# Narrow expert outputs summed in SBUF by one-hot products instead of scatters to HBM

## The chip, the core and the metric

The kernel runs on one core of a Trainium2 chip. The metric is the device time of one execution in microseconds (us); lower is better. The engines are TensorE (PE in the rows, with PEld for its weight loads), VectorE (DVE), ScalarE (ACT), GpSimd (POOL) and SyncE (SP). SP issues most transfers, POOL the indexed ones; all transfers run on the same 16 DMA engines.

## What is computed

One post-norm encoder layer over 512 tokens of width 1024: a token mixer, a cross-attention, and a mixture of experts. Only the last of these matters here:

```python
def moe(x, router_w, router_bias, e_w_gate, e_w_up, e_w_down, s_w_gate, s_w_up, s_w_down):
    scores = jax.nn.sigmoid((xf @ router_w).astype(jnp.float32))
    _, top_e = lax.top_k(scores + router_bias.astype(jnp.float32), TOP_K)   # 8 of 64 experts
    ...
    def body(acc, blk):
        rows, g, e = blk
        xb = x_pad[rows]
        yb = swiglu(xb, e_w_gate[e], e_w_up[e], e_w_down[e]) * g[:, None]
        return acc.at[rows].add(yb), None
    ...
    out = acc[:n] + swiglu(xf, s_w_gate, s_w_up, s_w_down)
...
h = layer_norm(ALPHA * h + y, ln3_g[l], ln3_b[l])
```

Every expert has three weight matrices of 1 MB (1024 x 256, 1024 x 256, 256 x 1024, float32), so 64 experts bring 192 MB from HBM.

## The kernel before

The experts are sorted by the number of their tokens. `CAPS` gives each rank a fixed number of rows: 128 for the first, two ranks with 160 (the "big" experts, which take two blocks, of 128 and of 32 rows), then 112, 96, 80, and for the last 26 ranks 64 (19 of them) and 48 (7). A block of at most 64 rows is *narrow*. All blocks run one after the other in the order of `seq`; `BIG_AT` says at which two places of that order the big experts stand.

For each block m, POOL gathers the token rows (`gather`, tile `xg`, two blocks ahead), PE transposes them (`rows_x`), multiplies them by gate and up weights, the gated product `hm` is transposed (`expert_h`, tile `ht`) and multiplied by the down weights `wd`, ScalarE copies the result to `y`, and POOL adds the rows of `y` to the sums `acc` in HBM with an indexed, adding transfer (`scatter`). Since all scatters write `acc`, each waits for the one before. The work is interleaved: within block m the down product of block m-1 is done, and the transposes of block m+1.

A wide block (over 64 rows) splits its weights and rows into high and low parts (tiles `whl`, `xt`; ScalarE and VectorE do the split) and multiplies three times in the fast form fp32r (`mm3`, lines 101 to 103). A narrow block multiplies unsplit float32 rows (`xn`) with gate and up side by side in two column halves of PE (`narrow_mm`, line 1280; `narrow_out`, line 1291).

Weights arrive through SP in the order of `seq`. `top_up` lets them be issued `LEAD` = 9 loads (three experts) ahead; each load takes one of 20 slots of 8 KB a partition, which weights, their split parts, outputs `y` and other large tiles share. At the end the four 128-row tiles of `acc` are read back into `h`, normalised and stored. A loop behind the blocks (line 1590) handles experts with more tokens than their rows; here it runs zero times.

The order of the instructions on each engine is fixed when the kernel is built: generators that yield estimated durations are interleaved, and within them a tile scheduler places the instructions.

## Time and profile before

| | |
|---|---|
| median of 3 runs | 1319.0 us (1314.91 to 1319.48) |
| profiled execution | 1310.08 us, of which the span from first to last instruction is 1308.3 us |
| busy share of the span | PE 88%, PEld 69%, DVE 57%, ACT 43%, POOL 34% |
| granted TensorE clock, mean | 0.963 of full speed |
| moved by DMA | 324.67 MB, mean 248 GB/s |
| queue q1 (loads and stores issued by SP) | 275.83 MB, 58.2% of 16 engines' span |
| queue q0 (issued by POOL) | 46.80 MB, 14.8% |

A busy share of PE counts a matmul from its start to a modelled end, so matmuls that follow each other overlap in it; starts are what a duration should be read from. The share of a DMA queue is the time that its packets took, as a share of the time of all 16 engines. The expert part begins near 596 us.

### The profile page before, as it was taken

To read this page: it belongs to the slowest core of one execution; us is meant where nothing else is said; L and a number is where in the kernel's file an instruction comes from. 1 tells how busy PE (TensorE), PEld (TensorE's weight loads), DVE (VectorE), ACT (ScalarE), POOL (GpSimd) and SP (SyncE) were. 2 spreads that over 40 slices of the span, in tenths; PEclk is the share of its full clock that TensorE was granted. 3 is DMA by queue.
4 is the path that set the end of the run, shared out by engine and by line. 5 is a ranking of instruction groups with operands and counts; after the bars stand their busy time and mean duration, and the time that the engine had idled before them with its cause. 6 is when DMAs were issued, how large, how long until landed. Compare 5 with 4: busy or idle time off the path is not lost. (4 is left out here: it accounts for less than half of the span.)

```text
span 1308.3 us, 20859 instructions
## 1 busy us (share of the span) xinstructions
PE 1155.8 (88%) x7768; PEld 908.2 (69%) x7768; DVE 748.5 (57%) x1617; ACT 562.0 (43%) x1006; POOL 439.5 (34%) x288
## 2 busy tenths in 40 slices
PE   3999999999898899889999999999899988897770
PEld 2887778988898898878778777777667544553330
DVE  7168986566865557787767777666465211311114
ACT  3235456644454453335555556555454211321122
POOL 4333444542236343552212323232213222223213
PEclk9999999998999899999999999999999989998995
DMA  7322234463326256688999999999999999999974
GB/s 225 86 74 65 58 103 114 121 202 116 126 67 210 63 185 208 226 332 329 299 289 331 352 347 362 332 359 359 350 367 338 350 347 387 363 363 353 349 279 141
DMA packets 136807, 324.67 MB, mean 248 GB/s; under 512 B 12001, under 2 KB 94945, under 8 KB 111873
## 3 DMA queue, kind: packets, MB, share of 16 engines
q1 hardware_dynamic: 119984, 275.83, 58.2%
q0 software_dynamic: 13632, 46.80, 14.8%
q8 instruction: 62, 1.02, 0.3%
q10 hardware_dynamic: 3088, 0.69, 0.2%
q14 instruction: 41, 0.33, 0.1%
HBM read 288.10 MB, written 35.19 MB: 247 GB/s over the span
## 5 line engine op out<-in xcount | busy, mean ns | idle before, releaser
L95 POOL TENSOR_TENSOR whl<-wraw,whl 128x1024 fp32r<-128x1024 f32 x81 | 195.9, 2419 | 265.4 <-ACT whl L94 239.4
L1244 DVE TENSOR_TENSOR whl<-wraw,whl 128x1024 fp32r<-128x1024 f32 x152 | 182.9, 1231 | 85.7 <-ACT whl L1243 79.6
L1332 POOL DMA_INDIRECT acc<-y,sidx x66 | 104.8, 1587 | 361.5 <-DMA acc<-y,sidx 161.4
L101 PE MATMUL ps<-whl,xt 128*96 128x256 f32 (+4 forms) x640 | 184.3, 288 | 5.6 <-ACT whl L1243 3.9
L103 PE MATMUL ps<-whl,xt 128*96 128x256 f32 (+4 forms) x640 | 179.8, 281 | 1.9 <-DVE xt L95 1.9
L102 PE MATMUL ps<-whl,xt 128*96 128x256 f32 (+4 forms) x640 | 179.6, 281 | 0.6 <-DVE whl L1244 0.6
L1243 ACT CAST whl<-wraw 128x1024 fp32r<-128x1024 f32 x152 | 152.5, 1053 | 27.9 <-DMA wraw<-in_e_w_gate_dram 20.0
L1327 PE MATMUL ps<-wd,ht 128*96 128x512 f32 (+4 forms) x320 | 147.1, 603 | 4.0 <-DVE ht L1315 3.8
L1280 PE MATMUL ps<-wraw,xn 128*64 128x256 f32 (+1 forms) x832 | 116.8, 404 | 27.0 <-DMA wraw<-in_e_w_up_dram 12.2
L1220 POOL DMA_INDIRECT xg<-rows,gidx x66 | 76.5, 1159 | 160.3 <-PE ps L1252 62.5
L1299 ACT ACTIVATE sg<-ps 64x256 f32<-64x256 f32 (+6 forms) x66 | 25.0, 378 | 239.6 <-PE ps L1280 127.1
L94 ACT CAST whl<-wraw 128x1024 fp32r<-128x1024 f32 x91 | 95.4, 1048 | 57.1 <-PE ps L103 46.5
L101 PEld LDWEIGHTS ps<-whl,xt 128*96 128x96 f32 (+4 forms) x640 | 104.3, 163 | 6.8 <-ACT whl L1243 4.1
L103 PEld LDWEIGHTS ps<-whl,xt 128*96 128x96 f32 (+4 forms) x640 | 104.3, 163 | 2.9 <-DVE xt L95 2.6
L1280 PEld LDWEIGHTS ps<-wraw,xn 128*64 128x64 f32 (+1 forms) x832 | 60.6, 140 | 65.0 <-DMA wraw<-in_e_w_up_dram 15.8
L102 PEld LDWEIGHTS ps<-whl,xt 128*96 128x96 f32 (+4 forms) x640 | 104.5, 163 | 1.1 <-DVE whl L1244 0.7
L1327 PEld LDWEIGHTS ps<-wd,ht 128*96 128x96 f32 (+4 forms) x320 | 49.5, 164 | 72.9 <-issue 66.0
L1315 DVE COPY ht<-ps 128x128 f32<-128x128 f32 (+6 forms) x66 | 21.4, 324 | 96.3 <-PE ps L1313 96.3
L1328 ACT COPY y<-ps 96x512 f32<-96x512 f32 (+4 forms) x80 | 46.3, 582 | 68.8 <-PE ps L1327 67.4
L1304 DVE SCALAR_TENSOR_TENSOR hm<-ps,og,sg 64x256 f32<-64x256 f32 (+4 forms) x54 | 36.8, 681 | 58.0 <-ACT sg L1299 48.8
L101 PE MATMUL ps<-xTh,whl 128*128 128x512 f32 (+1 forms) x168 | 65.6, 390 | 0.0
L103 PE MATMUL ps<-xTh,whl 128*128 128x512 f32 (+1 forms) x168 | 63.8, 380 | 0.0
(421 smaller groups left out, 2756.7 us busy)
## 6 DMA issues: line engine op xcount, KB each, us to landing
wraw<-in_e_w_gate_dram SPq DMA_DIRECT2D x64, 1024.0 KB, 18.8
wraw<-in_e_w_up_dram SPq DMA_DIRECT2D x64, 1024.0 KB, 15.7
wd<-in_e_w_down_dram SPq DMA_DIRECT2D x64, 1024.0 KB, 18.0
wraw<-in_w_in_dram SPq DMA_DIRECT2D x21, 512.0 KB, 3.7
wraw<-in_m_wkv_dram SPq DMA_DIRECT2D x16, 512.0 KB, 4.2
wraw<-in_m_wq_dram SPq DMA_DIRECT2D x16, 512.0 KB, 3.9
wraw<-in_m_wo_dram SPq DMA_DIRECT2D x16, 512.0 KB, 3.9
wraw<-in_w_o_dram SPq DMA_DIRECT2D x12, 512.0 KB, 3.5
```

The costliest lines, as they stand in the source:

```text
L94: nc.scalar.copy(hi, src)
L95: eng.tensor_sub(lo, src, hi.bitcast(F32))
L101: nc.tensor.matmul(ps, lhsT=a, rhs=b, start=start, stop=False)
L102: nc.tensor.matmul(ps, lhsT=a, rhs=bl, start=False, stop=False)
L103: nc.tensor.matmul(ps, lhsT=al, rhs=b, start=False, stop=stop)
L1220: nc.gpsimd.indirect_dma_start(out=xg[0:n, :], out_offset=None, in_=rows, in_offset=bass.IndirectOffsetOnAxis(ap=gi[0:n, :], axis=0))
L1243: nc.scalar.copy(hi[v], w[i][v])
L1244: lo_eng.tensor_sub(lo[v], w[i][v], hi[v].bitcast(F32))
L1280: nc.tensor.matmul(ps[HALF * i:HALF * i + n, 0:256], lhsT=xt[:, k, 0:n], rhs=w[i][:, k, :], start=k == 0, stop=k == KD - 1)
L1327: nc.tensor.matmul(ps[0:n, :], lhsT=ht[:, j, 0:n], rhs=wd[:, j, cs], start=j == 0, stop=j == 1)
L1328: nc.scalar.copy(y[0:n, cs], ps[0:n, :])
L1332: nc.gpsimd.indirect_dma_start(out=acc, out_offset=bass.IndirectOffsetOnAxis(ap=si[0:n, :], axis=0), in_=y[0:n, :], in_offset=None, comput ...
```

## The change

Three things change. The outputs of the narrow blocks no longer go to `acc` by scatters. Two consecutive narrow blocks form a pair: their outputs go to one tile `yp` (rows 0 to 63 and 64 to 127), as a high part (ScalarE) and the rest (VectorE); VectorE makes a one-hot matrix `ohs` of 128 rows by 512 tokens from the token numbers, and PE multiplies it with `yp` for each of 4 tiles of tokens and 2 column halves, two products each (high and rest), after which VectorE adds the result to the tile `sums` in SBUF. These 8 steps of a pair are spread over the two blocks behind it by `flush(2)`, called twice in a block. The sums are read once from `acc` (four loads of 0.5 MB, issued by POOL in the third narrow block, behind the last scatter of the wide blocks), and the final normalisation works on them directly. Seven slots are taken once for this and kept. The big experts move from places 30 and 50 to 22 and 32, so that all of the last 26 blocks are narrow. The lead of the weight loads is 10 instead of 9 in the narrow part.

```diff
@@ -38,7 +38,7 @@
 EARLY = 6
 FIRST_LOADS = ((("mo13",), 6), (("sh03",), 2), (("sh13",), 4))
 AHEAD, LEAD = 2, 9
-BIG_AT = (30, 50)
+BIG_AT = (22, 32)
 GRP = 4
 LO = (3, 0, 2, 0)
 PARTS = (2, 2)
@@ -1280,19 +1280,77 @@
                 nc.tensor.matmul(ps[HALF * i:HALF * i + n, 0:256], lhsT=xt[:, k, 0:n], rhs=w[i][:, k, :],
                                  start=k == 0, stop=k == KD - 1)

-    def narrow_out(m, ht, wd, n):
-
-        if m % 2 == 0:
-            Y["y"] = slot([P, 2, D], name="y")
-        y = Y["y"][:, m % 2, :]
+
+    ACC, YP, PAIR, STF, OHS, FL, READY = [], [], {}, {}, {}, [], []
+
+    def start_sums():
+
+        OHS[0] = ohs = slot([P, SEQ], F32R, name="tokens")
+        ohs = ohs[:, None, :]
+        ones_ = slot([P, 3, SEQ], F32R, name="ohs")
+        OHS[1] = [ones_[:, n, :] for n in range(3)]
+        YP.extend(slot([P, 2, D], F32R, name="yp") for _ in range(3))
+        tk = wk([P, SEQ], name="tk")
+        nc.gpsimd.iota(tk, pattern=[[1, SEQ]], base=0, channel_multiplier=0, allow_small_or_imprecise_dtypes=True)
+        nc.vector.tensor_copy(ohs[:, 0, :], tk)
+
+    def load_sums():
+        for u in range(2):
+            a = slot([P, 2, D], name="sums")
+            for t in range(2):
+                nc.gpsimd.dma_start(a[:, t, :], acc[(2 * u + t) * P:(2 * u + t + 1) * P, :])
+                ACC.append(a[:, t, :])
+
+    def one_hot_rows(oh, stf):
+        nc.vector.tensor_scalar(oh, OHS[0].bitcast(F32), stf, None, op0=OP.is_equal)
+
+    def add_sums(oh, yp):
+
+        for t in range(NT):
+            for c in range(2):
+                cs = slice(c * 512, (c + 1) * 512)
+                ps = bank()
+                for l in range(2):
+                    nc.tensor.matmul(ps, lhsT=oh[:, t * P:(t + 1) * P], rhs=yp[:, l, cs], start=l == 0, stop=l == 1)
+                nc.vector.tensor_add(ACC[t][:, cs], ACC[t][:, cs], ps)
+                yield
+
+    def narrow_out(m, ht, wd, n, si):
+
+        i = m - M0
+        p, base = i // 2, HALF * (i % 2)
+        if i % 2 == 0:
+            PAIR[p] = YP[p % 3]
+            STF[p] = small.tile([P, 1], F32, name="stf", bufs=3)
+            if min(blocks[m][2], blocks[m + 1][2]) < HALF:
+                nc.vector.memset(STF[p], -1.0)
+        yp, stf = PAIR[p], STF[p]
+        r = slice(base, base + n)
+        if n < HALF:
+            nc.gpsimd.memset(yp[base + 32:base + HALF].bitcast(F32), 0.0)
         ps = bank()
         for j in range(2):
             for c in range(2):
                 nc.tensor.matmul(ps[HALF * c:HALF * c + n, :], lhsT=ht[:, j, 0:n], rhs=wd[:, j, c * 512:(c + 1) * 512],
                                  start=j == 0, stop=j == 1)
-        for c in range(2):
-            nc.scalar.copy(y[0:n, c * 512:(c + 1) * 512], ps[HALF * c:HALF * c + n, :])
-        return y
+        nc.scalar.copy(stf[r], si[0:n])
+        halves = [(slice(c * 512, (c + 1) * 512), ps[HALF * c:HALF * c + n, :]) for c in range(2)]
+        for cs, v in halves:
+            nc.scalar.copy(yp[r, 0, cs], v)
+        for cs, v in halves:
+            nc.vector.tensor_sub(yp[r, 1, cs], v, yp[r, 0, cs].bitcast(F32))
+        if i % 2:
+            oh = OHS[1][p % 3]
+            one_hot_rows(oh, STF.pop(p))
+            READY.append(add_sums(oh, PAIR.pop(p)))
+
+    def flush(n):
+
+        while n and FL:
+            if next(FL[0], 0) == 0:
+                FL.pop(0)
+            else:
+                n -= 1

     def expert_gate(pg, n=P):
         sg = wk([P, 256], name="sg")
...
@@ -1463,7 +1523,8 @@

     def top_up(used):
         ahead = 16 + used // 2 if "listed" in done else 0
-        while fetched[0] < min(max(used + LEAD, ahead), 3 * NEXP):
+        lead = LEAD + (1 if used > 3 * step_of[blocks[M0][0]] else 0)
+        while fetched[0] < min(max(used + lead, ahead), 3 * NEXP):
             next(g_w)
             fetched[0] += 1

@@ -1480,11 +1541,11 @@

     def finish(m, ht, n, wd, si):
         if narrow(m):
-            y = narrow_out(m, ht, wd, n)
+            narrow_out(m, ht, wd, n, si)
         else:
             for c in range(2):
                 y = expert_out(m, ht, wd, c, n)
-        scatter(y, si, n)
+            scatter(y, si, n)

     def rows_x(m):
         return (narrow_x if narrow(m) else expert_x)(XG.pop(m), blocks[m][2])
@@ -1494,13 +1555,20 @@
     def narrow_block(m, X, xt, gs, si):
         r, _, n, _ = blocks[m]
         step = 3 * step_of[r]
+        if m == M0 + 1:
+            start_sums()
+        if m == M0 + 2:
+            load_sums()
         ps = bank()
         w = W[r]
+        FL.extend(READY)
+        READY.clear()
         narrow_mm(xt, w, n, ps, range(KH))
         yield 0.45 * KH, 0.0
         ht = expert_h(*BEFORE[0][0:2])
+        flush(2)
         narrow_mm(xt, w, n, ps, range(KH, KD))
-        yield 0.9, 0.0
+        yield 1.8, 0.0
         top_up(step + 2)
         sg = expert_gate(ps, n)
         finish(m - 1, ht, *BEFORE[0][1:])
@@ -1509,7 +1577,8 @@
         split_part(m + 1, 0)
         if m + 1 < NB:
             X[m + 1] = rows_x(m + 1)
-        yield 0.8, 0.0
+        flush(2)
+        yield 1.6, 0.0
         lists()
         lists()

@@ -1563,6 +1632,8 @@
         for _ in g_m:
             pass
         finish(NB - 1, expert_h(*BEFORE[0][0:2]), *BEFORE[0][1:])
+        FL.extend(READY)
+        flush(16)

     for u in range(2):
         items += [(load_half(w_o[0], 0, c), out_a(u, c), (f"so{4 * u + 3}",), f"oa{u}{c}", LO[0]) for c in range(4)]
...
+        oh, yp = OHS[1][0], YP[0]
+        one_hot_rows(oh, stf)
...
+            split(yp[:, 0, cs], yp[:, 1, cs], ps)
+        for _ in add_sums(oh, yp):
+            pass
...
     gb = G3[0]
-    h3 = [slot([P, 2, D], name="h") for _ in range(2)]
-    for t in range(NT):
-        nc.sync.dma_start(h3[t // 2][:, t % 2, :], acc[t * P:(t + 1) * P, :])
     st = []
     for t in range(NT):
-        h = h3[t // 2][:, t % 2, :]
+        h = ACC[t]
...
```

What this does to the order on two engines is shown here. PE, a narrow block near the end (before: one of the seven with 48 rows; L1268 transposes `xg`, L1280 gate and up, L1313 transposes `hm`, L1291 the down product of the block before; x counts instructions as written, and each float32 product has two rows in a trace):

```order
L1268 MATMUL ps<-ident,xg 128x48 x8
L1280 MATMUL ps<-wraw,xn 48x256
L1313 MATMUL ps<-ident,hm 128x48 x2
L1291 MATMUL ps<-wd,ht 48x512 x3
L1280 MATMUL ps<-wraw,xn 48x256 x15
L1291 MATMUL ps<-wd,ht 48x512
```

The same in the changed kernel, where L1371 stands for L1313, L1334 for L1291, and L1314 is a one-hot product:

```order
L1268 MATMUL ps<-ident,xg 128x48 x8
L1314 MATMUL ps<-yp,ohs 128x512 x4
L1280 MATMUL ps<-wraw,xn 48x256
L1371 MATMUL ps<-ident,hm 128x48 x2
L1314 MATMUL ps<-yp,ohs 128x512 x4
L1334 MATMUL ps<-wd,ht 48x512 x3
L1280 MATMUL ps<-wraw,xn 48x256 x15
L1334 MATMUL ps<-wd,ht 48x512
```

Eight one-hot products are added to a block, four behind the transposes and four behind the transposed `hm`. In this form, with three quarters of the down product ahead of 15 of the 16 gate and up products, stand the last 13 of the 26 narrow blocks. The ones ahead of them have this form:

```order
L1268 MATMUL ps<-ident,xg 128x64 x8
L1314 MATMUL ps<-yp,ohs 128x512 x4
L1280 MATMUL ps<-wraw,xn 64x256 x12
L1371 MATMUL ps<-ident,hm 128x64 x2
L1314 MATMUL ps<-yp,ohs 128x512 x4
L1280 MATMUL ps<-wraw,xn 64x256 x4
L1334 MATMUL ps<-wd,ht 64x512 x4
```

Here the down product comes last, behind all 16 gate and up products.

VectorE, a narrow block before (`hm` the gated product, `xn` half of the next block's rows, `ht` the transposed `hm`, `og` the gates and the expert's number for a later block):

```order
L1304 SCALAR_TENSOR_TENSOR hm<-ps,og,sg 64x128x2
L1406 COPY og<-gsl 64x1
L1408 COPY og<-order 1x1
L1315 COPY ht<-ps 128x2x64
L1271 COPY xn<-ps 128x256
```

and one of the late ones in the changed kernel, up to the next block's `hm`:

```order
L1362 SCALAR_TENSOR_TENSOR hm<-ps,og,sg 64x128x2
L1271 COPY xn<-ps 128x256
L1315 TENSOR_TENSOR sums<-sums,ps 128x512
L1341 TENSOR_TENSOR yp<-ps,yp 64x512 x2
L1315 TENSOR_TENSOR sums<-sums,ps 128x512
L1305 TENSOR_SCALAR ohs<-tokens,stf 128x512
L1373 COPY ht<-ps 128x2x64
L1466 COPY og<-gsl 48x1
L1315 TENSOR_TENSOR sums<-sums,ps 128x512 x2
L1468 COPY og<-order 1x1
L1326 MEMSET stf 128x1
```

Between `hm` and `ht` of a block there stand now two additions to the sums, two rests of `yp`, and in every second block the one-hot matrix.

On POOL the last scatter is that of the last wide block; the four loads of `sums` follow it with one gather between, and behind them there are only gathers and a few memsets.

## Rows read from the trace of the kernel before

**Rows 1.** Windows: busy us of each engine, granted clock, DMA share, GB/s

```profile
866.00:906.00 40.00, 36.40 (x256) 27.46 (x255) 24.89 (x47) 19.03 (x29) 14.71 (x8) 1.00 1.02 355
...
700.00:1007.00 307.00, 296.08 (x2040) 227.04 (x2038) 201.75 (x379) 164.85 (x250) 87.97 (x58) 0.99 1.02 352
1007.00:1272.00 265.00, 223.08 (x1508) 118.96 (x1506) 51.91 (x154) 58.01 (x121) 62.35 (x52) 0.94 1.00 352
...
1250.00:1252.00 2.00, 1.71 (x16) 0.78 (x12) 0.00 (x0) 0.26 (x1) 0.00 (x0) 1.00 1.03 430
```

**Rows 2.** PE in order of time: the gathered rows' transposes as the narrow part begins, and last

```profile
1007.49 0.71 PE L1268 MATMUL ps<-ident,xg 64*128 64x64 f32 x8
...
1035.95 0.71 PE L1268 MATMUL ps<-ident,xg 64*128 64x64 f32 x8
...
1258.89 0.69 PE L1268 MATMUL ps<-ident,xg 48*128 48x48 f32 x8
```

**Rows 3.** End of the narrow part in order of time: start, us, engine, line

```profile
1266.43 0.38 ACT L1299 ACTIVATE sg<-ps 48x256 f32<-48x256 f32 x1 [2.27 <-PE ps L1280]
...
1268.23 1.92 PE L1291 MATMUL ps<-wd,ht 128*48 128x512 f32 x8 [0.35 <-DVE ht L1315]
...
1281.80 1.35 POOL L1332 DMA_INDIRECT acc<-y,sidx  x1 [3.41 <-DMA acc<-y,sidx]
...
1289.92 1.28 DVE L171 BATCH_NORM_STATS2 st<-h 128x6 f32<-128x512 f32 x2 [21.74 <-DMA h<-acc]
```

**Rows 4.** DMA of 1040 to 1260 us: queue, packets, MB, share of 16 engines; issues

```profile
q1 hardware_dynamic: 9424, 68.64, 80.9%
q0 software_dynamic: 3439, 11.21, 21.1%
...
acc<-y,sidx POOLq DMA_INDIRECT x22, 8.3
xg<-rows,gidx POOLq DMA_INDIRECT x21, 8.8
```

**Rows 5.** PE in order of time: a big expert's blocks, from transposes to transposes

```profile
917.89 1.04 PE L1252 MATMUL ps<-ident,xg 128*128 128x128 f32 x8
...
928.78 0.68 PE L1252 MATMUL ps<-ident,xg 32*128 32x32 f32 x8
...
939.14 0.72 PE L1252 MATMUL ps<-ident,xg 80*128 80x80 f32 x8
```

**Rows 6.** PE in order of time: a narrow block that waits for no weights

```profile
1182.49 2.81 PE L1280 MATMUL ps<-wraw,xn 128*64 128x256 f32 x24 [0.26 <-ACT xn L1273]
...
1186.41 1.89 PE L1291 MATMUL ps<-wd,ht 128*64 128x512 f32 x8
...
1189.19 0.43 PE L1280 MATMUL ps<-wraw,xn 128*64 128x256 f32 x1 [0.26 <-ACT xn L1273]
```

**Rows 7.** PE in order of time: fp32r products of 512 columns in a row

```profile
261.22 0.40 PE L102 MATMUL ps<-aT,vb 128*128 128x512 f32 x1
261.45 0.39 PE L103 MATMUL ps<-aT,vb 128*128 128x512 f32 x1
```

**Rows 8.** DVE by line and shape: count, busy us, mean ns of one

```profile
L1304 DVE SCALAR_TENSOR_TENSOR hm<-ps,og,sg 64x256 f32<-64x256 f32 x19 | 12.8, 672 | 24.7 <-ACT sg L1299 24.6
...
L1271 DVE COPY xn<-ps 128x256 f32<-128x256 f32 x19 | 8.1, 424 | 47.9 <-PE ps L1268 47.9
...
L1315 DVE COPY ht<-ps 128x128 f32<-128x128 f32 x19 | 5.5, 291 | 61.5 <-PE ps L1313 61.5
...
L95 DVE TENSOR_TENSOR xTl<-ps,xTh 128x512 fp32r<-128x512 f32 x8 | 5.3, 680 | 0.0
...
L627 DVE TENSOR_SCALAR pa<-pa,r 128x512 f32<-128x512 f32 x8 | 5.2, 656 | 0.2
```

**Rows 9.** POOL in order of time: scatters as the narrow part begins

```profile
1021.78 1.43 POOL L1332 DMA_INDIRECT acc<-y,sidx  x1 [0.87 <-DMA acc<-y,sidx]
...
1032.41 1.43 POOL L1332 DMA_INDIRECT acc<-y,sidx  x1 [3.01 <-DMA acc<-y,sidx]
```

More of the change, by code (lines that the diff above doesn't have):

```diff
@@ L1395, in encoder_layer @@
     NB = len(blocks)
+    M0 = min(m for m in range(NB) if blocks[m][2] <= HALF and not blocks[m][1])
+    assert all(blocks[m][2] <= HALF and not blocks[m][1] for m in range(M0, NB)) and (NB - M0) % 2 == 0
     W, XG, GS = {}, {}, {}
@@ L1616, in encoder_layer @@
         ht = expert_h(expert_mid(expert_gate(pg), pu, gs))
+        stf = small.tile([P, 1], F32, name="stf", bufs=3)
+        nc.vector.tensor_copy(stf, si)
+        oh, yp = OHS[1][0], YP[0]
+        one_hot_rows(oh, stf)
         for c in range(2):
-            y = expert_out(0, ht, w3[2], c)
-        scatter(y, si)
+            cs = slice(c * 512, (c + 1) * 512)
+            ps = bank()
+            for j in range(2):
+                nc.tensor.matmul(ps, lhsT=ht[:, j, :], rhs=w3[2][:, j, cs], start=j == 0, stop=j == 1)
+            split(yp[:, 0, cs], yp[:, 1, cs], ps)
+        for _ in add_sums(oh, yp):
+            pass
     gb = G3[0]
-    h3 = [slot([P, 2, D], name="h") for _ in range(2)]
-    for t in range(NT):
-        nc.sync.dma_start(h3[t // 2][:, t % 2, :], acc[t * P:(t + 1) * P, :])
     st = []
     for t in range(NT):
-        h = h3[t // 2][:, t % 2, :]
+        h = ACC[t]
         if t % 2:
@@ L1634, in encoder_layer @@
     for t in range(NT):
-        h = h3[t // 2][:, t % 2, :]
+        h = ACC[t]
         mu, rs = st[t]
```

## Prediction

> **What bounds the kernel now.** I read the windows first. From 700 to 1007 us, where the wide blocks run, PE is busy for 296 of 307 us; from 1007 to 1272 us, the narrow part, for 223 of 265, while the DMA engines' share is 1.00 and the clock falls to 0.94 [rows 1]. So the wide part is bound by PE, though DMA is full there too, and the narrow part by DMA. The starts of the transposes give the narrow part's frame: the first at 1007.49, the fourth at 1035.95, the last at 1258.89 [rows 2]; the last down product ends at 1270.15, and from there it is 38.1 us to the end of the span: scatters that wait for each other, the last issued at 1281.80, the read-back of `acc`, and the normalisation from 1289.92 on, 18.4 us [rows 3].
>
> How long an expert takes on DMA: between 1040 and 1260 us q1 had 80.9% of 220 us, 178 us, for 68.64 MB, which is 386 GB/s, so the 3.146 MB of an expert cost 8.15 us; q0 had 46.4 us for 22 scatters and 21 gathers [rows 4]. If a gather of 64 rows (0.26 MB) goes at 386 GB/s, it costs 0.68 us and a scatter 1.46; at worst for the change both cost 1.08. PE needs less: an undisturbed narrow block goes from 1182.49 to 1189.19, 6.7 us [rows 6].
>
> **The change, part by part.**
>
> *The big expert's move.* Of the two big experts one stood among the narrow blocks, where PE had time left. Now both stand among the wide ones, where it has none. The other one's two blocks took from 917.89 to 939.14, 21.2 us [rows 5]; I take 21. So the first narrow transposes come at 1028.5. DMA gains about 7 us of lead by it (8.15 for the weights, 5 to 6 for gathers and scatters of 160 rows, against 21). Part of it pays where PE lost 3.6 of 40 us from 866 on [rows 1], which I put down to late weights: I take 2 back, with 0 and 4 as bounds.
>
> *The scatters.* 26 of them go, about 35 us of all DMA engines (28 if gathers and scatters cost alike). An expert then needs 8.15 + 0.68 = 8.8 us, or 9.2 at worst; the shares of both queues add up to 1.02, so 8.6 to 9.0. It cannot be the whole gain, because PE and VectorE get the work.
>
> *PE.* Eight more products of 512 columns a block. The rows have no such product with a one-hot matrix; the nearest is fp32r of the same size, which starts every 0.23 us though each lasts 0.39 [rows 7]. So 1.9 us a block, and 6.7 becomes 8.6, the same as DMA. If they didn't overlap it would be 3.1, and 9.8.
>
> *VectorE.* Each block gets four additions to the sums, two rests of `yp`, and half a one-hot matrix. The nearest rows are 680 ns (512 columns from PSUM) and 656 ns (a scalar operation in SBUF) [rows 8]. Per block that is 6 x 0.68 and 0.33, beside the 1.4 of `hm`, `xn` and `ht` that were there before: 5.8 us, less than 8.6. As a share it is no bound. But the order makes it a chain in the last 13 blocks, where three quarters of the down product stand ahead of 15 of 16 gate and up products. Follow one from the end of those products: silu 0.38 on ScalarE [rows 3], `hm` 0.67, `xn` 0.42, addition 0.68, two rests 1.36, addition 0.68, half a one-hot 0.33, `ht` 0.29 [rows 8]: then PE may start the down product, three quarters of 1.89 are 1.42, and 15/16 of the gate and up products (24 in 2.81 us, so 32 in 3.75) are 3.5 [rows 6]. That is 9.7 us, and each step waits for the one before; with some 0.3 for handing over I take 10.0 for a late block. Bounds: 8.6, if VectorE's run hid entirely, and 10.6. In the earlier form the down product is last, and `ht` is needed only after all the gate and up products; the chain is hidden there, and the block takes 8.6.
>
> *The load of the sums.* It waits for the last wide scatter, which was at 1021.78 and let the next go at 1032.41 [rows 9]; shifted by 21. The first addition needs its first quarter some 9 us later (the fourth transposes [rows 2] and about 5 us of products). 2.1 MB take 5.4 us of all engines at 386 GB/s; if each quarter took the 10.6 us of that scatter, one after the other, every one would come 2 to 3 us later than wanted. So 0 to 10 us; I take 2, as the four are issued together. The Trainium skill ("DMA: Bandwidth & Descriptors", Queues, rings and completion order) says that a DMA engine goes round between the queues that have work; by that the load would get half the engines beside the weights and land in an estimated 11 us, and the stall would be about the 2 us that I take. No run here shows it yet.
>
> *The end.* Nothing is scattered or read back. After the last down product come two copies and two rests (about 2 us, as ScalarE's copies and VectorE's rests overlap), then eight additions, 5.4, behind a first product; with 0.7 for the loop's branch that is 8.3, and 18.4 for the normalisation as before: 26.7 instead of 38.1.
>
> *The sum.* 1028.5, 28.5 for the first three blocks as before, 2 for the load: 1059. Ten blocks at 8.6: 1145. Twelve at 10.0: 1265, the last transposes. Before it was 11.3 from there to the end of the down product; with 1.9 of products and the VectorE run ahead of the last `ht` (four operations, 2.7 us, less what overlaps) 15.4: 1280.4. Plus 26.7, 1307; less 2 for the weights, 1305. The span was 1308.3, so the change is worth -3 us. The profiled execution took 1310.08, 9 us less than the median of 1319.0; I take the difference off the median: **1316 us**, no change. (A timing here can't tell less than about 0.5%, 6.6 us, from none.)
>
> **The rivals.**
>
> *Faster: VectorE's run is hidden in the late blocks too,* which then go at 8.6: 12 x 1.4 = 17 us less, 1299. For it: VectorE is busy 5.8 of 8.6 us, and the products' start is all that PE waits for. Against it: the order, in which `ht` stands behind five or six operations. At 9.3, half way, it is 1308, still faster. Chance 0.36.
>
> *Slower: the chain holds in the early blocks as well,* or the products don't overlap there (9.8): at 10.0, ten blocks cost 14 us more, 1330. For it: some of these blocks have four rests in a row ahead of an `ht`. Against it: `ht` has the time of 4 to 16 products there. It decides from a mean of 9.8 us over the 22 blocks (forecast 9.4). Chance 0.21.
>
> *DMA stays the bound,* because what is limited is the bytes and not the engines' time. The mean of the narrow part is 352 GB/s [rows 1]; 3.41 MB an expert without the scatter would take 9.7 us, ten early blocks 11 us more: 1327. Against it: 430 GB/s from 1250 to 1252 us, where loads had the engines to themselves [rows 1]. Chance 0.08. The Trainium skill ("DMA: Bandwidth & Descriptors", Where 436 GB/s comes from) has such a rule: for transfers between HBM and SBUF, HBM's share of a core, some 358 GB/s, binds. By it an expert would take an estimated 9.5 us and the time would be about 1325; the trace's 430 GB/s disagrees.
>
> **How the numbers follow.** No change (1312 to 1326) as reckoned has 0.35. Faster is the first rival, 0.36; slower is the second and half of the third, 0.25; the other half of the third ends within the bound, so same has 0.39. The range goes from the first rival to the second, with the bounds of the weights' 2 us and of the load's 2 us on either side: 1296 to 1333; the likeliest case alone has 1310 to 1325.
>
> **What would show it.** Right: first narrow transposes near 1028; early blocks 8.5 to 9 us apart and late ones near 10, PE waiting at L1334 for `ht` (L1373); SP's queue no longer the last in the narrow part, DMA share below 1 in the late blocks; no scatter behind 1055; some 27 us from the last down product to the end. Wrong: late blocks at 9 us or less (then 1300), early ones near 10 (1330), PE waiting for `wraw` all through (DMA still bounds), or a wait of over 5 us for `sums` on VectorE.

## Result and the profile after

The change made the kernel slower: 1340.1 us (median of 4, 1336.0 to 1342.1) against 1319.2 (1314.9 to 1319.5), a ratio of 1.0163 with a 95% interval of 1.0128 to 1.0197. The profiled execution of after took 1336.0 us, its span is 1334.2. The forecast was 1316, at most 1333.

The windows of the kernel after (columns as in [rows 1]), over the wide part, the narrow part, and ten of its microseconds:

```profile
700.00:1038.00 338.00, 323.93 (x2237) 249.02 (x2236) 216.47 (x420) 177.28 (x275) 87.86 (x62) 0.98 0.99 340
1038.00:1281.00 243.00, 229.69 (x1478) 127.14 (x1476) 132.86 (x266) 50.38 (x120) 38.92 (x37) 0.99 0.95 347
1160.00:1170.00 10.00, 9.44 (x61) 5.48 (x59) 5.70 (x13) 2.30 (x6) 0.89 (x1) 1.00 1.01 373
```

And its transposes of gathered rows, as in [rows 2]: the first, fourth, fourteenth and last narrow block.

```profile
1038.55 0.70 PE L1268 MATMUL ps<-ident,xg 64*128 64x64 f32 x8
...
1065.24 0.71 PE L1268 MATMUL ps<-ident,xg 64*128 64x64 f32 x8
...
1154.25 0.71 PE L1268 MATMUL ps<-ident,xg 64*128 64x64 f32 x8
...
1280.64 0.70 PE L1268 MATMUL ps<-ident,xg 48*128 48x48 f32 x8
```

PE is busy for 230 of the narrow part's 243 us; it was 223 of 265 [rows 1]. It waits for no weights there. So the bound did move from DMA to PE. Put beside the forecast's own terms, in us of the profiled execution:

| term | forecast | after |
|---|---|---|
| first narrow transposes (2 for early weights taken off) | 1026.5 | 1038.55 |
| three blocks, with the sums' load | 30.5 | 26.7 |
| ten early blocks | 86 | 89.0 |
| twelve late blocks | 120 | 126.4 |
| last transposes to last down product's end (1297.05) | 15.4 | 16.4 |
| from there to the end | 26.7 | 37.2 |
| sum | 1305.1 | 1334.2 |

The error is 12 us ahead of the narrow part, 6 in the late blocks and 10.5 at the end; the other terms nearly cancel. Each has a place in the trace. Of the 12 us, 6.5 come from ahead of the expert part, where the change does nothing. These are the first transposes of the experts, in the kernel before and then in the kernel after:

```profile
596.09 1.04 PE L1252 MATMUL ps<-ident,xg 128*128 128x128 f32 x8
```

```profile
602.57 1.04 PE L1252 MATMUL ps<-ident,xg 128*128 128x128 f32 x8
```

In the traces of kernels that are alike up to there they come anywhere from 595.9 to 606.3 us. From these transposes to the first narrow ones it is 411.4 us before and 436.0 after, 24.6 more, where 19 were forecast (21 less the 2).

**The wide part:** rows of several engines in order of time, behind the big expert at place 22. The product at 862.81 is PE's last one ahead of a wait.

```profile
859.35 1.45 POOL L1390 DMA_INDIRECT acc<-y,sidx  x1 [8.37 <-ACT xt L94]
...
862.81 0.28 PE L103 MATMUL ps<-whl,xt 128*96 128x256 f32 x1
869.67 3.88 ACT L1243 CAST whl<-wraw 128x1024 fp32r<-128x1024 f32 x4 [10.67 <-DMA acc<-y,sidx]
870.29 1.58 POOL L1390 DMA_INDIRECT acc<-y,sidx  x1 [8.28 <-DMA acc<-y,sidx]
870.75 1.23 DVE L1244 TENSOR_TENSOR whl<-wraw,whl 128x1024 fp32r<-128x1024 f32 x1 [10.48 <-ACT whl L1243]
...
872.81 0.42 PE L1371 MATMUL ps<-ident,hm 32*128 32x32 f32 x2 [9.71 <-DVE sidx L1185]
```

ScalarE's cast of the next expert's weights waits 10.67 us until a scatter has landed, the one issued at 859.35, which takes as long as that of [rows 9]; VectorE stands behind the cast, and PE behind VectorE, 9.7 us. From 860 to 880 us PE is busy for 10.3 of 20, at a granted clock of 0.66. The kernel before has the same wait, half as long, behind its big expert at place 30. Its rows stand just behind the last one of [rows 5], which is at 939.14:

```profile
946.64 3.88 ACT L1243 CAST whl<-wraw 128x1024 fp32r<-128x1024 f32 x4 [5.40 <-DMA acc<-y,sidx]
...
949.77 0.42 PE L1313 MATMUL ps<-ident,hm 32*128 32x32 f32 x2 [4.71 <-DVE sidx L1185]
```

**The late blocks:** the down product's wait for `ht` in a calm block, and then in one where GpSimd zeroes unused rows of `yp`.

```profile
1231.45 1.06 PE L1334 MATMUL ps<-wd,ht 128*48 128x512 f32 x4 [0.56 <-DVE ht L1373]
...
1238.72 3.65 POOL L1330 MEMSET yp<- 32x2048 f32 x2
...
1240.94 1.72 DVE L1305 TENSOR_SCALAR ohs<-tokens,stf 128x512 fp32r<-128x512 f32 x1
1242.58 0.24 DVE L1373 COPY ht<-ps 128x96 f32<-128x96 f32 x1
...
1242.87 1.84 PE L1334 MATMUL ps<-wd,ht 128*48 128x512 f32 x5 [2.02 <-DVE ht L1373]
```

The one-hot matrix takes 1.72 us there and ends 0.3 us behind the zeroing; PE waits 2.0 us instead of 0.6. Three late blocks are so drawn out, to 13.0, 13.1 and 11.4 us. In the first two the granted clock falls behind the wait (0.83 over 1220 to 1230 and over 1240 to 1250 us), in the third it stays at 1.00. **The end:**

```profile
1294.21 2.84 PE L1334 MATMUL ps<-wd,ht 128*48 128x512 f32 x8 [2.32 <-DVE ht L1373]
1296.98 6.46 PE L1314 MATMUL ps<-yp,ohs 128*128 128x512 f32 x24
...
1300.39 6.66 DVE L1315 TENSOR_TENSOR sums<-sums,ps 128x512 f32<-128x512 f32 x11
...
1309.28 1.29 DVE L171 BATCH_NORM_STATS2 st<-sums 128x6 f32<-128x512 f32 x2 [2.22 <-ACT sq L263]
...
1322.30 1.53 POOL L186 TENSOR_TENSOR sums<-sums,gb 128x512 f32<-128x512 f32 x1 [2.13 <-ACT sums L185]
...
1322.81 1.56 DVE L188 SCALAR_TENSOR_TENSOR sums<-sums,rs,gb 128x512 f32<-128x512 f32 x1
```

The rows answer to [rows 3]. From the down product's end to the first statistics are 12.2 us (forecast 8.3: four additions of the pair before were still to be made, 2.7 us, and the branch costs 2.2); the normalisation's 15.1 are nearly as before (14.7); and from VectorE's last operation to the end of the span 9.8 (3.7 before). What takes that time is a drain of GpSimd in the program's last line, in the after kernel (start and end of the group in us, duration in ns: least, median, most)

```profile
L1746 POOLq DRAIN  x3: 46/104/11135, 1322.3 to 1334.0; - x3
```

and in the kernel before:

```profile
L1669 POOLq DRAIN  x3: 46/104/4055, 1301.3 to 1308.0; - x3
```

It begins with GpSimd's last addition, at 1322.3, and ends 9.6 us after that is done. Before, it was 2.1.

### The profile page after: what moved, and what is told of

It is laid out like the page before. It is cut to its first block, busy times and chain, and to the rows that moved or that the text cites. A ratio compares the mean times of both kernels' runs of the same rounds, so it can differ in the third digit from the quotient of the medians.

```text
span 1334.2 us, 21444 instructions
## 1 busy us (share of the span) xinstructions
PE 1209.6 (91%) x7976; PEld 947.2 (71%) x7976; DVE 856.3 (64%) x1791; ACT 568.2 (43%) x1032; POOL 409.6 (31%) x274
## 5 line engine op out<-in xcount | busy, mean ns | idle before, releaser
L1220 POOL DMA_INDIRECT xg<-rows,gidx x66 | 70.9, 1074 | 304.8 <-PE ps L1268 142.3
L1390 POOL DMA_INDIRECT acc<-y,sidx x40 | 65.4, 1635 | 208.2 <-ACT whl L1243 58.1
L1280 PE MATMUL ps<-wraw,xn 128*64 128x256 f32 (+1 forms) x832 | 116.2, 388 | 1.6 <-ACT yp L1339 1.0
L1280 PEld LDWEIGHTS ps<-wraw,xn 128*64 128x64 f32 (+1 forms) x832 | 64.6, 134 | 41.6 <-issue 11.0
L1334 PE MATMUL ps<-wd,ht 128*64 128x512 f32 (+1 forms) x208 | 67.0, 625 | 14.4 <-DVE ht L1373 12.8
L1315 DVE TENSOR_TENSOR sums<-sums,ps 128x512 f32<-128x512 f32 x104 | 68.0, 682 | 17.6 <-PE ps L1314 12.6
L101 PE MATMUL ps<-xTh,whl 128*128 128x512 f32 (+1 forms) x168 | 67.3, 401 | 0.0
```

The source lines that it names most:

```text
L101: nc.tensor.matmul(ps, lhsT=a, rhs=b, start=start, stop=False)
L1220: nc.gpsimd.indirect_dma_start(out=xg[0:n, :], out_offset=None, in_=rows, in_offset=bass.IndirectOffsetOnAxis(ap=gi[0:n, :], axis=0))
L1280: nc.tensor.matmul(ps[HALF * i:HALF * i + n, 0:256], lhsT=xt[:, k, 0:n], rhs=w[i][:, k, :], start=k == 0, stop=k == KD - 1)
L1315: nc.vector.tensor_add(ACC[t][:, cs], ACC[t][:, cs], ps)
L1334: nc.tensor.matmul(ps[HALF * c:HALF * c + n, :], lhsT=ht[:, j, 0:n], rhs=wd[:, j, c * 512:(c + 1) * 512], start=j == 0, stop=j == 1)
```

## Experiments

Ratios are to the kernel before on the same chip, with 95% intervals; a run without one is a single execution, whose trace is what counts.

**1. The big experts' move.** In the kernel before, alone:

```
-BIG_AT = (30, 50)
+BIG_AT = (22, 32)
```

> The kernel before, with only the big experts' places changed to 22 and 32; scatters and read-back stay. Theory A (the move is paid in the wide part and only partly given back): the first narrow transposes come near 1038 us as in the changed kernel, with PE idle some 10 us around 860 and a slow clock behind it, and the narrow part is about 22 us shorter (30.6 us across the big expert become one block of 8.7): about 9 us longer than before, 1328. Theory B (DMA is busy from 700 us to the end, so only the sum of the bytes counts): the narrow part gets shorter by as much as the wide part gets longer, 1319, no change. Theory C (the move is worth nothing bad; the whole loss lies in the sums): 1310 to 1319 and first narrow transposes by 1030.

1328.7 us, 1.0085 (1.0053 to 1.0117), first narrow transposes at 1038.75: theory A, though what lies behind them is 13 us shorter and not 22 (288.0 against 300.8). The wide part is 435.5 us long, as in the changed kernel. This row of PE's waits from 700 to 1300 us (us in total, times, longest; line numbers of the kernel before) shows the same stall in a kernel that has nothing else of the change:

```profile
PE ps L1313 <- DVE sidx L1185: 9.4, 1, 9.4
```

So about half of the loss (0.85 of 1.63%) has nothing to do with the sums. Next, other places, and the other order of a big expert's blocks, both in the changed kernel:

```
-BIG_AT = (22, 32)
+BIG_AT = (30, 36)
```

> The changed kernel with the big experts at places 30 and 36 of the order instead of 22 and 32. Theory A (the stall of 10.7 us at 859 us is that of weights whose load SP issued late, behind the short block of the big expert at place 22, and belongs to that place): PE loses 5 us or less at the big experts, the first narrow transposes come at 1029 to 1032, and the time is 6 to 10 us shorter than the changed kernel's, 1330 to 1334. Rival (every big expert among the wide ones makes such a stall wherever it stands): two stalls or one of the same length, 1340 to 1346.

```
-        blocks.append((r, 0, min(CAPS[r], P), r))
         if CAPS[r] > P:
             blocks.append((r, P, CAPS[r] - P, NEXP + r - FIX))
+        blocks.append((r, 0, min(CAPS[r], P), r))
...
-        if m < NB and not narrow(m) and not blocks[m][1] and not isinstance(W[blocks[m][0]][i], tuple):
+        if m < NB and not narrow(m) and not isinstance(W[blocks[m][0]][i], tuple):
```

> The changed kernel with the two blocks of a big expert in the other order: the 32 rows first, the 128 rows behind them. Theory A (the stall of 9.7 us at 862 us is the load of the following expert's up weights: SP waits for a slot that the big expert's split weights hold until the short block's last product, and PE has only some 2 us of work left while the load takes 8.7): with the long block last the load has that block's time, PE's wait at the first big expert falls below 3 us, the first narrow transposes come near 1030 us and the time is 8 to 10 us shorter than the changed kernel's, 1330 to 1332. Rival (DMA is simply late by that much, wherever the blocks stand): PE waits as long, at this place or some experts later, 1338 to 1342.

1336.6 (1.0133, 1.0094 to 1.0171) and 1338.8 (1.0157, 1.0122 to 1.0192). The stall stays: 7.1 us behind place 30, 8.9 with the short block first. So it is not that SP's load has too little time behind a short block; that theory fell. What the cast waits for is told by the order of the program after, on ScalarE (DMASW are GpSimd's transfers, DMAHW SP's):

```
674 L1243 CAST whl_9332<-wraw_8961 128x1024 [waits DMAHW7_49,Activation_49]
679 L1243 CAST whl_9400<-wraw_9001 128x1024 [waits DMASW6_49,DMAHW0_49,DMASW4_49,Activation_49]
```

The first is an ordinary cast, which waits for its weights. The second, the first one behind the big expert, also waits for two of GpSimd's transfers: its slot held `y` before, and `y` is free only when its scatters have landed. The 20 slots go round. Two ordinary blocks take 15 of them (twice 3 loads and 4 halves of split weights, and one `y`), and then the turn of `y`'s old slot falls on a load, so that SP waits, which has a lead (SP waits 107 us for scatters from 700 to 1035 us, and PE for no weights). The two blocks of a big expert take 8, the turn shifts, and it falls on a cast: ScalarE waits, which has none. This count of slots is worked out from the kernel, not traced, and it leaves open why the second big expert makes no such stall, or less of one. If it is right, taking `y` out of the ring takes the stall away, weights late or not:

```
-    slots = ctx.enter_context(tc.tile_pool(name="slots", bufs=20))
+    slots = ctx.enter_context(tc.tile_pool(name="slots", bufs=18))
+    ys = ctx.enter_context(tc.tile_pool(name="ys", bufs=2))
...
-            Y["y"] = slot([P, 2, D], name="y")
+            Y["y"] = ys.tile([P, 2, D], F32, tag="y", name="y")
...
-            a = slot([P, 2, D], name="sums")
+            a = ys.tile([P, 2, D], F32, tag="y", name="sums")
```

> The changed kernel with y in two buffers of its own, which the sums take over later, and 18 slots instead of 20. Theory A (ScalarE's cast of the next expert's weights waits for a slot in which y lay, until its scatter has landed, 10.7 us): with no y in the ring PE's wait at the first big expert falls below 3 us, SP no longer waits for scatters in the wide part, the first narrow transposes come at 1026 to 1030 and the time is 8 to 12 us shorter than the changed kernel's. Rival (the weights themselves are late, since DMA has no time left in the wide part): ScalarE waits as long for wraw, first narrow transposes at 1035 or later, 1336 to 1342.

1329.1 us, 1.0065 (1.0042 to 1.0087): 11 us below the changed kernel. First narrow transposes at 1031.7; the wide part takes 429.7 us, where the traces of all kernels with `y` in the ring and the big experts at 22 and 32 have 435.5 to 443.9. PE has no wait of over 0.6 us from 700 us on, except one of 1.4 us for `flagb`, which the changed kernel has too, and ScalarE's waits for split weights from 700 to 1035 us are these, none for a scatter:

```profile
ACT whl L1244 <- PE ps L103: 4.4, 2, 2.4
ACT whl L1244 <- DVE whl L1245: 0.8, 2, 0.5
```

The transposes come 2 us later than theory A said, from experts that start at 602.0. Part of the gain is given back: PE waits 6.0 us in the narrow part for gathered rows (experiment 5).

**2. The late blocks.** The zeroing left out:

```
-        if n < HALF:
-            nc.gpsimd.memset(yp[base + 32:base + HALF].bitcast(F32), 0.0)
```

> The changed kernel without the zeroing of the unused rows of yp (GpSimd), whose old rows meet zeros of the one-hot matrix. Theory A (while GpSimd zeroes 2 x 1.8 us, VectorE's one-hot matrix takes 1.72 us instead of 0.48, ht comes 1.2 us later, PE waits 2.0 us and its clock falls behind that): the three blocks of 13.0, 13.1 and 11.4 us take 9.8, and the time falls by 6 to 8 us, to 1333. Rival (PE's waits there are covered by the weights, which could not come faster): the blocks stay above 11 us or PE waits for wraw, 1338 to 1341.

1332.3, 1.0105 (1.0067 to 1.0144), 8 us less; the intervals overlap by a little, and the traces are what shows the cause. The three blocks take 10.2 each, and the mean of the twelve is 10.0, the forecast's number. The one-hot matrix in the changed kernel and then without the zeroing (ns: least, median, most):

```profile
L1305 DVE TENSOR_SCALAR ohs<-tokens,stf x13: 476/481/1720, 1070.4 to 1263.7; 128x512 fp32r<-128x512 f32 x13
```

```profile
L1305 DVE TENSOR_SCALAR ohs<-tokens,stf x13: 477/479/485, 1072.3 to 1259.5; 128x512 fp32r<-128x512 f32 x13
```

Then the chain itself, with all four additions behind `ht`:

```
         ht = expert_h(*BEFORE[0][0:2])
-        flush(2)
+        flush(4)
...
             X[m + 1] = rows_x(m + 1)
-        flush(2)
```

> The changed kernel with the four additions of a block all behind the copy to ht in VectorE's queue (two of them stood ahead of it). Theory A (the late blocks are a chain through VectorE: hm, xn, addition, two rests, addition, ht): without the two additions and the one-hot matrix in it the chain is covered by PE's eight one-hot products, the twelve late blocks take 8.7 to 8.9 us instead of 10.5, PE has no wait for ht of over 0.5 us, and the time falls by 18 to 22 us, to about 1320. Rival (DMA is the bound, at about 9.7 us an expert): the late blocks take 9.6 or more, PE waits for wraw, and the time falls by 10 us at most, 1330 or more. Rival (the products don't overlap): no change, 1338 to 1342.

1336.8, 1.0124 (1.0084 to 1.0165): a miss of theory A by 17 us. PE no longer waits for `ht`, but 18 of the 22 blocks take 9.5 to 9.9, early ones too (the others 8.8, 10.3, 12.4 and 13.6). In one of them, in order of time:

```profile
1194.58 1.18 ACT L1339 CAST yp<-ps 64x512 fp32r<-64x512 f32 x2 [1.31 <-PE ps L1334]
...
1195.78 0.37 ACT L1273 COPY xn<-ps 128x256 f32<-128x256 f32 x1
...
1196.20 2.81 PE L1280 MATMUL ps<-wraw,xn 128*64 128x256 f32 x24 [1.03 <-ACT xn L1273]
```

A new wait, once a block: `xn` stands behind the casts to `yp` on ScalarE. Without it that block is 9.55 - 1.03 = 8.5, PE's own work. The next kernel has no zeroing, has `ht` first, and writes the transposes of the next rows ahead of the down product, which is in `finish`:

```
         sg = expert_gate(ps, n)
+        if m + 1 < NB:
+            X[m + 1] = rows_x(m + 1)
         finish(m - 1, ht, *BEFORE[0][1:])
...
         split_part(m + 1, 0)
-        if m + 1 < NB:
-            X[m + 1] = rows_x(m + 1)
```

> The changed kernel with three edits: no zeroing; the four additions behind the copy to ht; the next rows' transposes written ahead of the down product, so that ScalarE's copy of xn is no longer awaited behind its casts to yp (1.03 us of PE a block with the additions behind ht alone). Theory A (the narrow block's floor is PE's own work, 8.5 us: 0.7 transposes, 3.65 gate and up, 0.3, 2.0 one-hot products, 1.85 down): all 22 blocks behind the third take 8.5 to 8.8 us, and the time falls to 1310 to 1316. Rival (DMA at 8.6 to 9.0 an expert becomes the bound): blocks at 9.0, PE waits for wraw, 1316 to 1322. Rival (another wait of the chain takes their place): blocks at 9.5 or more, 1328 or more.

1321.9, 1.0038 (1.0004 to 1.0072), 18 us below the changed kernel, but 6 above the range of theory A. The late blocks take 8.3 and 10.3 by turns, most of them. In every second one PE waits for the high parts (ScalarE) and the rests (VectorE) of the pair that it is about to add:

```profile
1252.25 0.50 PE L1314 MATMUL ps<-yp,ohs 128*128 128x512 f32 x1 [0.41 <-ACT yp L1337]
...
1253.57 2.16 PE L1314 MATMUL ps<-yp,ohs 128*128 128x512 f32 x7 [0.82 <-DVE yp L1339]
```

So a pair's additions are put one block later, and two of GpSimd's additions at the end go to VectorE (experiment 4):

```
-        FL.extend(READY)
+        FL.extend(LATER)
+        LATER[:] = READY
         READY.clear()
+        if m == NB - 1:
+            FL.extend(LATER)
+            LATER.clear()
...
-            scale_add(v, v, rs, b, c == 0)
+            scale_add(v, v, rs, b, c == 0 and t < 2)
```

> The kernel with the three edits (no zeroing, additions behind ht, next rows' transposes earlier), and two more: a pair's additions start one block later, and the last two additions of the normalisation go from GpSimd to VectorE. Theory A (in every second late block of that kernel PE waits 1.2 us for the rests of the pair that it is to add, and the block takes 10.3 instead of 8.3): the late blocks take 8.3 to 8.5 each, 10 to 12 us less in all, and the end is 2 to 5 us shorter: 1306 to 1312. Rival (DMA binds at 8.6 to 9 us an expert when PE no longer does): blocks near 9 with PE waiting for wraw, 1312 to 1318.

1311.2, 0.9941 (0.9915 to 0.9966): this form beats the kernel before. The time is that of theory A; the late blocks are not, they take 8.3 to 10.0, and PE waits for weights again, 1.3 us in all. What each of the two new edits is worth by itself was not measured.

**3. What DMA allows.** The additions of twelve pairs left out:

```
-        FL.extend(READY)
         READY.clear()
```

> The changed kernel without the one-hot products and additions of twelve of the thirteen pairs (that part of the computation is left out); weights, gathers, rests and one-hot matrices stay. It shows what DMA alone allows without scatters. Theory A (DMA needs 8.6 to 9.0 us an expert, as its share of the engines says): PE needs about 7 us, waits for wraw, and the blocks settle at 8.6 to 9.0 us once the lead of 10 loads is used up. Rival (bytes bind, 9.7 us an expert): blocks settle at 9.6 or more. Rival (the chain through VectorE holds even without the additions): blocks at 9 or more with PE waiting for ht and not for wraw.

1314.9 us in a single execution. The 25 blocks from 1045.9 to 1264.1 take 8.7 us in the mean, eight in a row 8.3 to 8.4 and the others 5.0 to 13.7. PE waits for `wraw` for 4.1 us in all, and for `xn`, `hm` and `ht` for 23, so this is not the wait that theory A named. Its pace of DMA is right: from 1118 to 1262 us q1 moves 51.01 MB (packets, MB, share of the engines),

```profile
q1 hardware_dynamic: 7007, 51.01, 92.9%
```

which is 8.9 us for each expert's 3.146 MB. That is in theory A's 8.6 to 9.0, and 9.7 is out. A block of 8.5 us is thus a little faster than its weights; the loads' lead covers the difference.

**4. The end.** The sums loaded by SP; the last two additions on VectorE (`c == 0 and t < 2`, as above); one gather more ahead of the normalisation; each in the changed kernel:

```
-                nc.gpsimd.dma_start(a[:, t, :], acc[(2 * u + t) * P:(2 * u + t + 1) * P, :])
+                nc.sync.dma_start(a[:, t, :], acc[(2 * u + t) * P:(2 * u + t + 1) * P, :])
```

```
+    gather(gidx[:, 0:1])
     gb = G3[0]
```

> The changed kernel with the four loads of the sums issued by SP instead of GpSimd; nothing else is touched. In the changed kernel, in the one without zeroing and in the one with the additions behind ht, GpSimd's last drain took 11.13 us, against 4.06 and 4.09 us in the two kernels with scatters at the end, and the span ends 7.1 us after the last output packet, against 1.4. Theory A (the drain waits for what the plain loads left in GpSimd's own queue): the drain takes about 4 us, the span ends about 1.5 us after the last packet, and the time falls by 6 us to about 1334; the loads in SP's queue, behind a wait for the last scatter, hold the weights up by less than 3 us. Rival (the drain belongs to the instructions at the end, whatever was loaded): 11.1 us again, 1338 to 1342. Rival (SP's queue stands still for the scatter and the weights come late): the drain is short but PE waits for wraw by 4 us or more in the first narrow blocks, 1337 or more.

> The changed kernel with the last two of GpSimd's four additions in the normalisation given to VectorE. GpSimd's last drain took 10.8 to 11.1 us in all six kernels without a scatter at the end, and 4.1 us in the two with one. Theory A (the drain is a fixed time that starts with GpSimd's last instruction and only shows because that comes late): it still takes 11.1 us, but begins 3 to 5 us earlier against VectorE's last operation, and the span ends 2 to 5 us behind the last output packet instead of 7.1. Rival (it waits for something that ends at a fixed place, such as the output): the span ends 7 us behind the last packet again.

> The changed kernel with one gather of 128 rows more, behind the loop of late rows and ahead of the normalisation; nothing reads it. Theory A (the drain is short when an indirect transfer was issued from the last program part, long when the last one lay far back): the drain takes about 4 us and the span ends 1.5 us behind the last output packet, 5 us earlier. Rival (it has to do with the accumulating scatters, or with the kernel's end in some other way): 11.1 us again.

1333.8 (1.0137, 1.0083 to 1.0190), 1329.1 and 1328.5 us. In all three the drain ends 9.2 to 9.7 us behind GpSimd's last addition. So theory A fell in the first and the third: neither the queue of the sums' load nor a late gather shortens the drain. It held in the second: where GpSimd's last addition comes earlier, the end does too (SP is done 2.4 us before the end of the span, in the changed kernel 7.0). The drain's exact end depends on how many transfers GpSimd issued: 9.24 us with 112, 9.57 with 116, 9.65 with 117, 0.082 each. But the kernel before issues 138 and has 2.1. So 22 small loads were added, which makes 138 without a narrow scatter:

```
         lists()
         lists()
+        if m >= NB - 22:
+            nc.gpsimd.dma_start(small.tile([P, 1], F32, name="pad", bufs=4), col(ln3_g, P))
```

> The changed kernel with 22 small loads (128 numbers each) more in GpSimd's queue, one in each of the last 22 narrow blocks; nothing reads them. GpSimd then issues 138 transfers in all, as the kernel before does, of which none is a narrow scatter. Theory A (the drain costs 0.082 us for each transfer since some count was last reset, and the reset comes between 117 and 138): it ends about 2.1 us behind GpSimd's last instruction. Rival 1 (it costs 0.082 us for each, and scatters count differently): 11.4 us. Rival 2 (no connection with the number): 9.57 us.

```profile
L1748 POOLq DRAIN  x3: 46/104/3945, 1324.1 to 1329.6; - x3
```

The drain ends 2.4 us behind the last addition, and the span 3.7 us behind VectorE's last operation, as before (9.8 in the changed kernel). So it is not the scatters. The number of transfers fits; that the 22 loads come late was not tried apart from their number. The arithmetic of theory A does not come out: a count that starts anew behind 117 would leave at most 21 transfers, 1.7 us at 0.082 each.

**5. Versions built on it.** The kernel with three edits, with big experts at 10 and 16; the delayed additions with the short block first, with `y` outside the ring, that with the sums loaded by SP, and that with 26 small loads:

> The kernel with those three edits and the big experts at places 10 and 16 of the order. Theory A (the stall of 7 to 10 us is weights that come late behind the big expert's short block, because it holds its slots through two blocks while DMA has no time left): it stands at either place, and the time is within 4 us of the same kernel with places 22 and 32. Rival (at the earlier places DMA still has a lead and hides it): no wait of over 3 us at the big experts, 6 to 10 us shorter.

> The kernel with the delayed additions, and the big experts' short blocks ahead of their long ones. Theory A: another 8 to 10 us less by the stall at 862, 1297 to 1303, 1 to 1.5% faster than the kernel before. Rival (what the wide part gains the narrow part loses, since DMA is busy all along): within 3 us of the kernel with the delayed additions.

> The kernel with the delayed additions, and y in two buffers of its own as above. Theory A: 8 to 12 us below the kernel with the delayed additions, 1300 to 1304, over 1% faster than the kernel before. Rival (DMA late): no faster than that kernel, 1309 to 1314.

> The kernel with delayed additions and y in its own buffers, with the sums loaded by SP. Theory A (in that kernel PE waits 11.1 us for gathered rows, because the gather stands in GpSimd's queue behind the sums' load, which waits for the last scatter): that wait falls below 2 us and the time by 7 to 11 us, to 1291 to 1295. Rival (SP then stands still for that scatter and the weights come late): PE waits for wraw instead, 1299 to 1304.

> The last kernel with 26 small loads more in GpSimd's queue, one in each narrow block, 138 transfers from GpSimd in all. Theory A: GpSimd's drain ends about 2.1 us behind its last instruction, the span ends 1.5 us behind the last output packet, 2 us earlier than without them (the last two additions are on VectorE there, so only some 2 us of the drain show). Rival: no difference, or up to 2 us slower for the drain's longer count.

Places 10 and 16: 1329.3, 1.0081 (1.0048 to 1.0113), 7 us worse; the stall is 6.1 us behind place 10 and 1.5 or less behind 16, and the narrow part begins with weights that come late. Short block first: 1307.6, 0.9919 (0.9889 to 0.9948), with a stall of 8.7, so not by what was meant; it can't be told from the kernel without. `y` outside: 1301.8, 0.9867 (0.9842 to 0.9892), as expected. With SP: 1299.0, 0.9866 (0.9840 to 0.9891): PE's wait of 11.1 us for gathered rows is gone, but the ratio is the same, a miss of theory A. The narrow part begins 2.9 us later there (2.4 of it lie ahead of the experts), PE waits 3.4 us for weights, and some blocks take 8.8 to 12.8; what else took the gain back was not traced. The last blocks run at PE's floor, 8.5:

```profile
1221.12 0.90 PE L1269 MATMUL ps<-ident,xg 48*128 48x48 f32 x8
1229.59 0.91 PE L1269 MATMUL ps<-ident,xg 48*128 48x48 f32 x8
1238.07 0.90 PE L1269 MATMUL ps<-ident,xg 48*128 48x48 f32 x8
```

With the small loads: 1303.25, 0.9891 (0.9866 to 0.9917), no gain, though the drain does end 2.4 us behind GpSimd's last addition, and the span 1.3 us behind the last packet.

## Why the prediction was wrong

- *"Of the two big experts one stood among the narrow blocks ... I take 21."* This step failed. It took PE's time for a big expert's two blocks from [rows 5] and moved it. Those rows end at 939.14, and PE's wait behind a big expert, for a cast that waits for a scatter, comes at 945 to 950: 4.7 us in the kernel before, 9.7 after. The sum has no term for it, and does not ask how the move changes the order in which buffers go round. The wide part became 24.6 us longer in place of 19, and most of the 5.6 between is that this wait grew by 5.0. With `y` outside the ring the wide part is 18.3 longer than before (429.7 against 411.4), near the forecast. By the timing the ring is worth 11 us. The 2 us to be had back from early weights can't be read apart from this. The other 6.5 us of the first row of the table are not the change's.
- *The end, 26.7.* It failed by 10.5: 6.1 the drain, which stood in no row that I had read, because before it ended ahead of the last output; 2.7 four more additions; 1.5 the branch, for whose 0.7 the forecast named no row, and which took 2.2.
- *VectorE's chain in the late blocks, 10.0.* Right as a number: 10.0 without the zeroing, and PE waits at L1334 for `ht`. But that wait is 0.4 to 0.8 us in a calm block, less than the 1.4 by which the forecast's chain outlasts PE's work; what the rest is was not traced, and taking `ht` out of the chain brought most blocks to 9.5 to 9.9 and not to 8.7 (experiment 2). What was left out is the zeroing on GpSimd, which I gave no price: some 7 us in the profiled execution (126.4 against 119.4 for the twelve), 8 by the timing. The Trainium skill ("SBUF — State Buffer", Who interferes with whom) has the rule: VectorE and GpSimd share one pair of ports, and where a VectorE instruction uses that pair, as a scalar operation can, the one that comes second waits until the other's instruction is done. The trace agrees: the one-hot matrix from 1240.94 ends at 1242.66, the zeroing at 1242.37.
- *PE 8.6 a block, early blocks 8.6, products that overlap.* Right: 8.5 of own work; the early blocks take 8.6 to 8.8 but for three of 9.1 to 10.0 (mean 8.9); 24 one-hot products in 6.46 us start 0.26 apart (one lasts 0.39), not 0.23, at a granted clock of 0.88 there.
- *The load of the sums, 2 us.* PE did not wait for it at all; VectorE did, 1.1 and 2.6 us, in the shadow of PE's work. The load itself was slower than the estimate of 11 us: issued from 1064.11 on, a quarter of it was still waited for until 1081.77, 17 us later. The estimate gave it half of the bytes. From 1068 to 1082 us its queue q0 moved about as many packets as q1, but half-size ones (4 KB against 8), so a third of the bytes:

```profile
q1 hardware_dynamic: 538, 3.91, 67.4%
q0 software_dynamic: 515, 1.91, 34.1%
```

The Trainium skill ("DMA: Bandwidth & Descriptors", Queues, rings and completion order) has the engines go round between queues packet by packet, not byte by byte; the counts of this trace fit it, and it was the forecast that took this for equal bytes. The waits, in rows of the kernel after, in order of time:

```profile
1064.11 2.23 POOL L1301 DMA_DIRECT2D sums<-acc  x4 [3.67 <-DMA acc<-y,sidx]
...
1076.64 1.29 DVE L1315 TENSOR_TENSOR sums<-sums,ps 128x512 f32<-128x512 f32 x2 [1.10 <-DMA sums<-acc]
...
1081.77 1.28 DVE L1315 TENSOR_TENSOR sums<-sums,ps 128x512 f32<-128x512 f32 x2 [2.57 <-DMA sums<-acc]
```

- *"DMA share below 1 in the late blocks."* Wrong as a sign: the share is 1.01 from 1160 to 1170, and 1.02 from 1154 to 1240, while PE waits for no weights; it falls later, as the last loads land (0.81 from 1214 to 1280). The claim behind it, that DMA is no longer the bound, was right, and the rival of 9.7 us an expert fell with experiment 3.
- The rival on the slower side named a chain that holds in the early blocks too. That was not it: eight of the ten early blocks take 8.6 to 9.1. The time came out 10 us above even that rival's 1330, for reasons that none of the cases held.
- The frame: the profiled execution of before is 9 us below the median, that of after 4. The spans differ by 26 us, the medians by 21; what is worked out from the two traces is therefore too large by some 5 us in all. The later start of the experts, 6.5 us, is about that much. The lead of 10 loads was not tried by itself.

By runs the three things missing are worth 11 us (ring; 13 by the ratios), 8 (zeroing) and, by the trace alone, 6 (drain). Together they are 25, against an error of 24. That this fits so well is in part luck: the other terms of the table, the additions and the branch at the end included, come to some 5 us more, and the two by runs are uncertain by several us.

## What to carry to other kernels

Where all buffers come from one ring, a change in the order of the work changes who gets whose old buffer. Look up, on the engine that has no lead, which of its writes now wait for a transfer out of that buffer. When you take the price of moved work from rows, read on past its last row until the engine is back in step: here the wait stood just behind. When a bound moves from DMA to an engine, each wait removed lets the next one out (`ht`, then `xn`, then the rests); the gain came only when the last was gone. And price what the idle engine does too: its memory operation can hold another up, and its end is the kernel's end.

## What the runs showed of the hardware

- The drain at GpSimd's end takes 0.082 us for each transfer that GpSimd issued (112, 116 and 117: 9.24, 9.57, 9.65 us), and only 2.1 to 2.4 us with 138 (2.14 in the kernel before, 2.18 in experiment 1, 2.38 and 2.42 with small loads). Where between 118 and 138 it turns short, and why, stays open. What it saves in time was not shown: the one timing that could tell, the last version of experiment 5, where some 2 us of the drain show, has no gain.
- VectorE's one-hot matrix takes 0.48 us (I took 0.66), and 1.7 us beside GpSimd's zeroing; its additions from PSUM take 0.69 beside it as elsewhere.
